# Differential attention scores: the low-key pass on 64 partitions, both components in one run of four matmuls

## The chip, the cores and the metric

The kernel runs on one core of a Trainium2 chip. Its engines are TensorE (PE; its weight loads are shown as PEld), VectorE (DVE), ScalarE (ACT), GpSimd (POOL) and SyncE (SP, which here only issues transfers). The metric is the device time of one execution in microseconds (us).

## The reference

One encoder layer is applied to two sequences, of 1024 and of 256 tokens. A state-space branch and a differential-attention branch share one input projection, and their outputs are gated and merged. What the change touches is the attention:

```python
def block(qi):
    s = jnp.einsum('bqhtd,bkhtd->bthqk', qi, k).astype(jnp.float32) * scale
    p = jax.nn.softmax(s, axis=-1)
    w = p[:, 0] - lam * p[:, 1]
    return jnp.einsum('bhqk,bkhe->bqhe', w, v)
```

There are 4 heads. Each has two components t = 0, 1 of head dimension 64, and the two softmaxes are subtracted. Query blocks have 128 rows.

## The kernel before

Every 32-bit operand of a large matmul is split into a high part and a low part (a rounded copy, and what the rounding left). In DRAM, `q_d` and `k_d` hold both parts of the rotated queries and keys. `load_head(h)` brings one head into SBUF. A query tile (`q0` for t = 0, `q1` for t = 1) stacks the 64 high rows on partitions 0 to 63 and the 64 low rows on partitions 64 to 127. A key tile holds the same 64 key rows twice, once for each half of the queries: `k00`, `k01` hold the high parts, `k10`, `k11` the low parts. One matmul over 128 partitions so gives (high q + low q) times one part of k.

A unit is one query block of one head. `unit_scores` computes its two score tiles `S0` and `S1` (128 x 1024 in PSUM, one buffer each, two banks each). For each t there is a high pass (two matmuls of 512 columns, line 924) and a low pass (two more into the same banks, line 926). Then VectorE takes the row maximum (`mx`, line 928) and scales it (line 929), ScalarE forms the exponentials `p` with the row sum (line 932), which frees the score tile, and after both components VectorE and POOL combine them (lines 937 to 940). `unit_transpose` transposes the result on TensorE (line 949) and `pair_out` multiplies it with the values (lines 961 to 963). There are 8 long units per head (1024 keys) and 2 short ones (256 keys): 32 long and 8 short in all.

The projections that only later stages need are cut into 576 steps of three matmuls, the filler (lines 706 to 708). `fill(n, ins)` puts n steps behind the instruction `ins`. Steps that the state-space and attention stages don't take are done behind them, before the gated stages, so the total number of steps is fixed. In the attention stage the order on every engine is made by a scheduler at build time, from the program and its own planning, and each engine works through its order strictly.

Transfers into the head's tiles reuse the tags `U`, `tb`, `mt`, `wcm`, `wb`, which name the SBUF slots: in the profile's rows `hU`, `htb`, `hmt`, `hwcm`, `hwb`. `S<-hmt,hU` is the low pass of t = 0 and `S<-hwb,htb` that of t = 1.

Earlier, line 440 issues very small matmuls that use 32 columns of the array. The rows give the part of the array used as rows*columns: `128*32` there, `32*128` on lines 275 and 276, `128*128` nearly everywhere else.

Of the kernel before, what the change touches and what calls it, by code (L numbers as in the profile page):

```python
# [11 lines left out]
F32 = mybir.dt.float32  # L12
# [10 lines left out]
LL = 1024  # L23
LS = 256
NT = LL + LS
# [101 lines left out]
def kernel(  # L127
# [6 lines left out]
    V, G, A, PE, SP = nc.vector, nc.gpsimd, nc.scalar, nc.tensor, nc.sync  # L134
# [3 lines left out]
    def dram(shape, dtype, name):  # L138
        return tc.dram_tile(shape, dtype, name=name)
# [7 lines left out]
    q_d = [dram([2, 2, 128, NT], F32, f"q_d{i}") for i in range(2)]  # L147
    k_d = [dram([2, 2, 128, NT], F32, f"k_d{i}") for i in range(2)]
# [27 lines left out]
    def after(ins):  # L176
        return tc.issue_after(ins.ins) if ins else ExitStack()
# [543 lines left out]
    def fill(steps, ins=None):  # L721
        with after(ins):
            for _ in range(steps):
                next(filler, None)
# [4 lines left out]
    with ExitStack() as p2:  # L729
# [20 lines left out]
        def load_wb(b):  # L750
            wb = (sp_ if b % 2 else sl).tile([128, 2, NB, 128], F32, tag="wb", name="wb")
            SP.dma_start(wb, wb_d[b])
            return wb
# [81 lines left out]
        with tc.manual_schedule(engines={mybir.EngineType.PE, mybir.EngineType.SP}):  # L835
# [10 lines left out]
            for b in range(NBLK):  # L846
                q = b // 2
# [22 lines left out]
    with ExitStack() as p3:  # L870
        ap = p3.enter_context(tc.tile_pool(name="att", bufs=1, reuse_waits="tile"))
        ps_s = p3.enter_context(tc.tile_pool(name="ps_s", bufs=1, space=PSUM, reuse_waits="tile"))
# [3 lines left out]
        def load_head(h):  # L876
            pr, cb = h // 2, (h % 2) * 2
            big = lambda tag, b: sl.tile([128, NT], F32R, tag=tag, name=f"h{tag}", bufs=b)
            sml = lambda tag, b: sl.tile([128, LL], F32R, tag=tag, name=f"h{tag}", bufs=b)
            q0, k00, q1, vh = big("U", 2), big("tb", 2), big("tb", 2), big("U", 2)  # L880
            k10, k01, k11, vl, rest = sml("mt", 2), sml("wcm", 2), sml("wb", 1), sml("mt", 2), sml("wcm", 2)
            part = lambda i: rest[:, i * LS:(i + 1) * LS]
            v3 = lambda t: t.rearrange("p (k e) -> p k e", e=128)

            def load_q(t, q):
                rows = slice((cb + t) * 32, (cb + t) * 32 + 32)
                for s in range(2):
                    for f in range(2):
                        o = s * 64 + f * 32
                        SP.dma_start(q[o:o + 32].bitcast(F32), q_d[pr][s, f, rows])  # L890

            def load_k(t, hl, k, c0, n):
                rows = slice((cb + t) * 32, (cb + t) * 32 + 32)
                for s in range(2):
                    for f in range(2):
                        o = s * 64 + f * 32
                        SP.dma_start(k[o:o + 32].bitcast(F32), k_d[pr][hl, f, rows, c0:c0 + n])

            load_q(0, q0)
            load_k(0, 0, k00, 0, NT)  # L900
            load_k(0, 1, k10, 0, LL)
            load_q(1, q1)
            load_k(1, 0, k01, 0, LL)
            load_k(1, 1, k11, 0, LL)
            SP.dma_start(v3(vh).bitcast(F32), vh_d[h])
            SP.dma_start(v3(vl).bitcast(F32), vl_d[h][:, 0:8])
            load_k(0, 1, part(0), LL, LS)
            load_k(1, 0, part(1), LL, LS)
            load_k(1, 1, part(2), LL, LS)
            SP.dma_start(v3(part(3)).bitcast(F32), vl_d[h][:, 8:10])  # L910
            return (([q0[:, :LL], q1[:, :LL]], [k00[:, :LL], k01], [k10, k11], v3(vh)[:, 0:8], v3(vl)),
                    ([q0[:, LL:], q1[:, LL:]], [k00[:, LL:], part(1)], [part(0), part(2)],
                     v3(vh)[:, 8:10], v3(part(3))))

        def unit_scores(hd, qi, nk, fu):
            qs, kh, kl = hd[:3]
            pt = []
            sm = ap.tile([128, 2], F32, tag="sm", name="sm", bufs=2)
            for t in range(2):
                S = ps_s.tile([128, LL], F32, tag=f"S{t}", name=f"S{t}")  # L920
                qw = qs[t][:, qi * 128:qi * 128 + 128]
                cks = [(c, min(512, nk - c)) for c in range(0, nk, 512)]
                for c, n in cks:
                    PE.matmul(S[:, c:c + n], qw, kh[t][:, c:c + n], start=True, stop=False)  # L924
                for c, n in cks:
                    last = PE.matmul(S[:, c:c + n], qw, kl[t][:, c:c + n], start=False, stop=True)  # L926
                mx = ap.tile([128, 1], F32, tag=f"mx{t}", name=f"mx{t}", bufs=2)
                V.tensor_reduce(mx, S[:, :nk], axis=AX.X, op=ALU.max)  # L928
                V.tensor_scalar(mx, mx, -1.0 / math.sqrt(HD), None, op0=ALU.mult)  # L929
                p = ap.tile([128, LL], F32, tag=f"p{t}", name=f"p{t}", bufs=3 - t)  # L930
                with tc.issue_after(tables.ins):
                    A.activation(p[:, :nk], S[:, :nk], AF.Exp, bias=mx, scale=1.0 / math.sqrt(HD),  # L932
                                 accum_out=sm[:, t:t + 1])
                pt.append(p)
                fill(fu[t], last if fu[t] else None)
            rs = ap.tile([128, 2], F32, tag="rs", name="rs", bufs=2)
            V.reciprocal(rs, sm)  # L937
            V.tensor_tensor(rs[:, 1:2], rs[:, 1:2], nlam, op=ALU.mult)
            G.tensor_scalar(pt[0][:, :nk], pt[0][:, :nk], rs[:, 0:1], 1.0, op0=ALU.mult, op1=ALU.mult)  # L939
            V.scalar_tensor_tensor(pt[0][:, :nk], pt[1][:, :nk], rs[:, 1:2], pt[0][:, :nk], op0=ALU.mult, op1=ALU.add)  # L940
            return pt[0]
# [71 lines left out]
        for h in range(NH):  # L1013
            parts = load_head(h)
            for pi in range(5):
                nk = LL if pi < 4 else LS
                fl = F_LONG if pi < 4 else F_SHORT
                hd = parts[pi // 4]
                wTh = ap.tile([128, 8, 256], F32R, tag="wTh", name="wTh", bufs=2)
                wTl = ap.tile([128, 8, 256], F32R, tag="wTl", name="wTl", bufs=2)  # L1020
                for qi in range(2):
                    w = unit_scores(hd, (pi % 4) * 2 + qi, nk, fl)
                    if prev:
                        finish(prev, fl[2])
                    else:
                        fill(fl[2])
                    fill(fl[3])
                    prev = (h, pi, qi, w, hd, wTh, wTl)
# [123 lines left out]
    for grp in range(2):  # L1152
# [4 lines left out]
        wb = load_wb(0)  # L1157
        for f in range(8):
            bh, bl = wb
            if f < 7:  # L1160
                wb = load_wb(f + 1)
# [13 lines left out]
            last = split_into(mh[:, f], ml[:, f], s1)  # L1175
# [75 lines left out]
```

## Time and profile before

| | us |
|---|---|
| median of 3 runs (1124.25 to 1127.57) | 1126.07 |
| the profiled execution | 1127.2 |
| its span, first to last instruction | 1125.1 |
| TensorE busy | 1067.2 (95%) |
| VectorE busy | 801.0 (71%) |
| ScalarE busy | 462.5 (41%) |
| attention stage, about 457 to 778 | 321 |

The profiled execution is 2.1 us longer than its span, and 1.1 us above the median. A matmul's duration in the rows includes the time its result takes to come out. What a matmul costs in a packed stream is the distance from its start to the next start.

### The profile page before, as it was taken

The numbers are of one execution on the slowest core, as the hardware profiler recorded it, in microseconds if no ns is written. First come the engines' busy times: TensorE is split into PE (matmuls) and PEld (weight loads), VectorE is DVE, ScalarE is ACT, GpSimd is POOL, SyncE is SP. The second block draws the span as 40 slices with busy tenths as digits, with TensorE's granted clock in tenths as the row PEclk, the third lists the DMA queues.
The fourth block names the chain that finished last, engine by engine and source line by source line (L and its number), as shares of the span: only waits on it lengthen the run. The fifth ranks groups of instructions, "written<-read, shape, count | busy, mean of one in ns | idle before, by whom it ended". The sixth has DMA issues, their size and how long they took to land.

```text
span 1125.1 us, 18000 instructions
## 1 busy us (share of the span) xinstructions
PE 1067.2 (95%) x6479; PEld 987.1 (88%) x6479; DVE 801.0 (71%) x1533; ACT 462.5 (41%) x927; POOL 354.8 (32%) x437
## 2 busy tenths in 40 slices
PE   5999799999989999999999999999999999998997
PEld 4878588788979988898999998989999999998997
DVE  5998997888579999478677777766442675666524
ACT  4453222332312121455555645554453445544332
POOL 2447999511032333122122222212141003520032
PEclk9999899999999999999999999999999999999999
DMA  7745453654596676615416316311645975569112
GB/s 212 170 141 188 142 174 117 209 166 156 173 282 174 205 202 168 177 51 150 141 47 169 122 47 186 114 40 60 210 124 174 292 230 128 167 194 270 48 57 94
DMA packets 186154, 173.59 MB, mean 154 GB/s; under 512 B 32721, under 2 KB 161745, under 8 KB 186066
## 3 DMA queue, kind: packets, MB, share of 16 engines
q1 hardware_dynamic: 150738, 144.13, 43.6%
q10 hardware_dynamic: 35328, 28.32, 7.9%
q8 instruction: 51, 0.84, 0.3%
q14 instruction: 37, 0.30, 0.1%
HBM read 113.71 MB, written 58.69 MB: 153 GB/s over the span
## 4 chain that ended last, share of the span: by engine, by line
PE 47%; DVE 18%; DMA 7%; ACT 4%; issue 3%; POOL 2%; SPq 0%; ACTq 0%; POOLq 0%; DVEq 0%
PE mm L706 5%; PE mm L707 5%; PE mm L708 5%; PE xb L1058 3%; PE xb L1059 3%; PE xb L1060 3%; PE pb L246 2%; PE pb L248 2%; PE pb L247 2%; DVE z L797 2%; DVE z L798 2%; PE S L924 2%; DMA yt<-ya_d 2%; PE S L926 2%; DVE mx L928 2%
## 5 line engine op out<-in xcount | busy, mean ns | idle before, releaser
L706 PE MATMUL mm<-hTh,wh 128*128 128x424 f32 (+1 forms) x576 | 212.2, 368 | 6.3 <-ACT zo L712 6.3
L708 PE MATMUL mm<-hTh,wl 128*128 128x424 f32 (+1 forms) x576 | 206.1, 358 | 0.0
L707 PE MATMUL mm<-hTl,wh 128*128 128x424 f32 (+1 forms) x576 | 206.0, 358 | 0.0
L706 PEld LDWEIGHTS mm<-hTh,wh 128*128 128x128 f32 x576 | 109.2, 190 | 12.6 <-ACT zo L712 8.1
L707 PEld LDWEIGHTS mm<-hTl,wh 128*128 128x128 f32 x576 | 109.2, 190 | 4.6
L708 PEld LDWEIGHTS mm<-hTh,wl 128*128 128x128 f32 x576 | 109.0, 189 | 3.4
L928 DVE TENSOR_REDUCE mx<-S 128x1 f32<-128x1024 f32 (+1 forms) x80 | 84.2, 1057 | 38.9 <-PE S L926 38.7
L939 POOL TENSOR_SCALAR p<-p,rs 128x1024 f32<-128x1024 f32 (+1 forms) x40 | 41.7, 1042 | 205.0 <-DVE rs L937 194.2
L246 PE MATMUL pb<-hTh,wh 128*128 128x512 f32 (+1 forms) x288 | 105.7, 367 | 0.0
L247 PE MATMUL pb<-hTl,wh 128*128 128x512 f32 (+1 forms) x288 | 105.1, 365 | 0.0
L932 ACT ACTIVATE p<-S,mx 128x1024 f32<-128x1024 f32 (+1 forms) x80 | 79.2, 992 | 63.0 <-DVE mx L929 53.8
L248 PE MATMUL pb<-hTh,wl 128*128 128x512 f32 (+1 forms) x288 | 103.9, 361 | 0.4 <-DVE wl L240 0.4
L240 POOL TENSOR_TENSOR wl<-wst,wh 128x1024 fp32r<-128x1024 f32 x24 | 64.3, 2679 | 126.5 <-ACT wh L239 51.7
L1191 PE MATMUL tr<-wqh,mh 128*128 128x256 f32 x320 | 89.7, 280 | 1.5 <-DVE o L1195 1.3
L1192 PE MATMUL tr<-wql,mh 128*128 128x256 f32 x320 | 89.3, 279 | 0.0
L1193 PE MATMUL tr<-wqh,ml 128*128 128x256 f32 x320 | 89.0, 279 | 0.0
L248 PEld LDWEIGHTS pb<-hTh,wl 128*128 128x128 f32 x288 | 54.6, 190 | 9.3 <-DVE wl L240 0.9
L246 PEld LDWEIGHTS pb<-hTh,wh 128*128 128x128 f32 x288 | 54.7, 190 | 8.6
L1191 PEld LDWEIGHTS tr<-wqh,mh 128*128 128x128 f32 x320 | 60.1, 188 | 2.4 <-DVE o L1195 2.4
L247 PEld LDWEIGHTS pb<-hTl,wh 128*128 128x128 f32 x288 | 54.6, 190 | 8.4
L1198 POOL TENSOR_TENSOR o<-o,finB 128x256 f32<-128x256 f32 x30 | 27.9, 934 | 103.8 <-ACT jk L1197 103.8
L1192 PEld LDWEIGHTS tr<-wql,mh 128*128 128x128 f32 x320 | 60.1, 188 | 0.0
(387 smaller groups left out, 2793.4 us busy)
## 6 DMA issues: line engine op xcount, KB each, us to landing
wst<-in_w_in_dram ACTq DMA_DIRECT2D x24, 512.0 KB, 4.0
wst<-in_w_in_dram SPq DMA_DIRECT2D x16, 512.0 KB, 4.8
wst<-in_w_branch_dram SPq DMA_DIRECT2D x32, 256.0 KB, 4.4
wqs<-in_w_out_dram SPq DMA_DIRECT2D x16, 512.0 KB, 3.8
tt_d<-tt SPq DMA_DIRECT2D x16, 320.0 KB, 2.6
tb<-tt_d SPq DMA_DIRECT2D x8, 640.0 KB, 5.1
zt<-gs_d SPq DMA_DIRECT2D x16, 320.0 KB, 4.3
x<-in_x_sample_dram SPq DMA_DIRECT2D x8, 512.0 KB, 4.6
```

Of the source, the lines that this page charges most:

```text
L240: e.tensor_tensor(lv, st, hv, op=ALU.subtract)
L246: PE.matmul(ps[:, :n], wh[:, k, :], hTh[:, k, c0:c0 + n], start=(k == 0), stop=False)
L247: PE.matmul(ps[:, :n], wh[:, k, :], hTl[:, k, c0:c0 + n], start=False, stop=False)
L248: PE.matmul(ps[:, :n], wl[:, k, :], hTh[:, k, c0:c0 + n], start=False, stop=(k == KD - 1))
L706: PE.matmul(ps[:, :n], wh[:, k, :], hTh[:, k, c0:c0 + n], start=(k == 0), stop=False)
L707: PE.matmul(ps[:, :n], wh[:, k, :], hTl[:, k, c0:c0 + n], start=False, stop=False)
L708: PE.matmul(ps[:, :n], wl[:, k, :], hTh[:, k, c0:c0 + n], start=False, stop=(k == KD - 1))
L928: V.tensor_reduce(mx, S[:, :nk], axis=AX.X, op=ALU.max)
L932: A.activation(p[:, :nk], S[:, :nk], AF.Exp, bias=mx, scale=1.0 / math.sqrt(HD), accum_out=sm[:, t:t + 1])
L1191: PE.matmul(ps[:, :256], mh[:, k, ts_], oh_[:, k], start=(k == 0), stop=False)
L1192: PE.matmul(ps[:, :256], mh[:, k, ts_], ol_[:, k], start=False, stop=False)
L1193: PE.matmul(ps[:, :256], ml[:, k, ts_], oh_[:, k], start=False, stop=(k == 7))
```

## The change

The low pass of the long units leaves out the product of the low queries with the low keys. It uses the high queries only, so 64 partitions of operands instead of 128. Its four matmuls (two halves of the keys for each of two components) are put on alternating halves of the partitions: keys 0 to 511 on partitions 0 to 63, keys 512 to 1023 on partitions 64 to 127. The high passes of both components come first, then the four low matmuls in one run, held behind the last high matmul. The filler of both components now waits for the last low matmul. Short units keep their 128-partition low pass.

For this `load_head` builds other tiles. `klo` (slot `mt`) has the low keys of both components once each, split over the partition halves. The high queries must stand on both halves, so `q1` is stacked the other way round (low rows first), and `qx` (slot `wb`) holds the two missing copies.

```diff
-            k10, k01, k11, vl, rest = sml("mt", 2), sml("wcm", 2), sml("wb", 1), sml("mt", 2), sml("wcm", 2)
+            klo, k01, qx, vl, rest = sml("mt", 2), sml("wcm", 2), sml("wb", 1), sml("mt", 2), sml("wcm", 2)
...
+            def load_klo(t):
+                rows = slice((cb + t) * 32, (cb + t) * 32 + 32)
+                for s in range(2):
+                    for f in range(2):
+                        o = s * 64 + f * 32
+                        SP.dma_start(klo[o:o + 32, t * 512:t * 512 + 512].bitcast(F32),
+                                     k_d[pr][1, f, rows, s * 512:s * 512 + 512])
+
-            load_q(0, q0)
+            load_q(0, q0, 0, 0)
+            load_q(0, q0, 64, 1)
             load_k(0, 0, k00, 0, NT)
-            load_k(0, 1, k10, 0, LL)
-            load_q(1, q1)
+            load_klo(0)
+            load_q(0, qx, 64, 0, LL)
+            load_q(1, q1, 64, 0)
+            load_q(1, q1, 0, 1)
             load_k(1, 0, k01, 0, LL)
-            load_k(1, 1, k11, 0, LL)
+            load_klo(1)
+            load_q(1, qx, 0, 0, LL)
...
+            his = ((q0[0:64], qx[64:128]), (qx[0:64], q1[64:128]))
+            los = [[(his[t][s], klo[64 * s:64 * s + 64, t * 512:t * 512 + 512]) for s in range(2)] for t in range(2)]
...
-            for t in range(2):
-                S = ps_s.tile([128, LL], F32, tag=f"S{t}", name=f"S{t}")
+            cks = [(c, min(512, nk - c)) for c in range(0, nk, 512)]
+            Ss = [ps_s.tile([128, LL], F32, tag=f"S{t}", name=f"S{t}") for t in range(2)]
+            for t, S in enumerate(Ss):
                 qw = qs[t][:, qi * 128:qi * 128 + 128]
-                cks = [(c, min(512, nk - c)) for c in range(0, nk, 512)]
                 for c, n in cks:
-                    PE.matmul(S[:, c:c + n], qw, kh[t][:, c:c + n], start=True, stop=False)
-                for c, n in cks:
-                    last = PE.matmul(S[:, c:c + n], qw, kl[t][:, c:c + n], start=False, stop=True)
+                    hi_last = PE.matmul(S[:, c:c + n], qw, kh[t][:, c:c + n], start=True, stop=False)
+                if nk < LL:
+                    last = PE.matmul(S[:, :nk], qw, kl[t], start=False, stop=True)
+            if nk == LL:
+                for t, S in enumerate(Ss):
+                    for (c, n), (qh_, kl_) in zip(cks, kl[t]):
+                        with after(hi_last):
+                            last = PE.matmul(S[:, c:c + n], qh_[:, qi * 128:qi * 128 + 128], kl_, start=False, stop=True)
+            for t, S in enumerate(Ss):
                 mx = ap.tile([128, 1], F32, tag=f"mx{t}", name=f"mx{t}", bufs=2)
```

The order on TensorE at the fifth long unit of the first head, before. `S_5307` is its S0 and `S_5338` its S1; `tr<-ident,p` are the transposes of an earlier unit.

```order
L924 MATMUL S_5307<-htb,hU 128x512 x2
L926 MATMUL S_5307<-hmt,hU 128x512 x2
L949 MATMUL tr<-ident,p_5147 128x128 x8
...
L924 MATMUL S_5338<-hwcm,htb 128x512 x2
L926 MATMUL S_5338<-hwb,htb 128x512 x2
```

The same unit in the changed kernel, where `S_5311` is S0 and `S_5312` is S1, the high pass is line 936 and the low pass line 943.

```order
L936 MATMUL S_5311<-htb,hU 128x512 x2
L936 MATMUL S_5312<-hwcm,htb 128x512 x2
L943 MATMUL S_5311<-hmt,hU 128x512
L943 MATMUL S_5311<-hmt,hwb 128x512
L943 MATMUL S_5312<-hmt,hwb 128x512
L943 MATMUL S_5312<-hmt,htb 128x512
L706 MATMUL mm<-hTh,wh 128x424
```

The two components stood 8 transposes and 18 filler matmuls apart and now stand together, with the low pass of both behind them. From the low pass of S_5311 to the next unit's S0 there are now 21 filler matmuls, 8 transposes and two matmuls of the normalization; before, from the low pass of S_5307, there were 8 transposes, 18 and then 3 filler matmuls, the four matmuls of S_5338 and the same two of the normalization.

VectorE at the same unit, before: the row maximum of S0 (`mx_5312`), its scaling, and what stands up to the maximum of S1 (`mx_5343`).

```order
L928 TENSOR_REDUCE mx_5312<-S_5307 128x1
L929 TENSOR_SCALAR mx_5312<-mx_5312 128x1
L937 RECIPROCAL rs<-sm 128x2
L938 TENSOR_TENSOR rs<-rs,nlam 128x1
L953 TENSOR_TENSOR wTl<-tr,wTh 128x4x128 x2
L940 SCALAR_TENSOR_TENSOR p_5244<-p_5270,rs,p_5244 128x1024
L928 TENSOR_REDUCE mx_5343<-S_5338 128x1
```

VectorE there in the changed kernel (`mx_5321` for S0, `mx_5347` for S1):

```order
L946 TENSOR_REDUCE mx_5321<-S_5311 128x1
L958 SCALAR_TENSOR_TENSOR p_5253<-p_5274,rs,p_5253 128x1024
L946 TENSOR_REDUCE mx_5347<-S_5312 128x1
L947 TENSOR_SCALAR mx_5321<-mx_5321 128x1
L971 TENSOR_TENSOR wTl<-tr,wTh 128x4x128
```

The scaling of S0's maximum, for which ScalarE's exponentials wait, stood right behind the maximum and now stands behind the combination of the unit before and behind the maximum of S1.

SP's queue where the second head is loaded, in the changed kernel. Before, 12 transfers of 32x1024 (`hmt`, `hwcm` and `hwb`, four each) stood ahead of the `ya_d` store.

```order
L895 DMA hwcm<-k_d_91 32x1024 x2
L902 DMA hmt<-k_d_91 32x512 x4
L888 DMA hwb<-q_d_89 32x1024 x2
L895 DMA hwcm<-k_d_91 32x1024 x2
L902 DMA hmt<-k_d_91 32x512 x4
L888 DMA hwb<-q_d_89 32x1024
L1015 DMA ya_d_95<-ya 128x512
L888 DMA hwb<-q_d_89 32x1024
L895 DMA htb<-k_d_91 32x1280
```

There are 16 transfers in place of 12 between the head's last long unit and the loads that wait for its short units, and one of them stands behind the `ya_d` store.

## Rows read from the trace of the kernel before

**Rows 1.** Attention stage: stretch, its length, busy us per engine (instructions), clock, DMA.

```profile
457.00:778.00 321.00, 312.24 (x1821) 289.87 (x1821) 234.51 (x425) 172.31 (x351) 73.25 (x52) 0.99 0.37 108
```

**Rows 2.** Timeline, PE, second head: start, us, engine, line, operation.

```profile
596.00 0.62 PE L924 MATMUL S<-htb,hU 128*128 128x512 f32 x2
596.47 0.62 PE L926 MATMUL S<-hmt,hU 128*128 128x512 f32 x2
596.93 0.35 PE L706 MATMUL mm<-hTh,wh 128*128 128x432 f32 x1
597.12 0.36 PE L707 MATMUL mm<-hTl,wh 128*128 128x432 f32 x1
```

**Rows 3.** All low passes of long units (line 926): count, ns min/median/max, starts.

```profile
L926 PE MATMUL S<-hmt,hU x64: 387/396/628, 458.1 to 759.5; 128*128 128x512 f32 x64
L926 PE MATMUL S<-hwb,htb x64: 387/394/403, 461.3 to 762.8; 128*128 128x512 f32 x64
```

**Rows 4.** Timeline, PE, around one run of the 32-column matmuls.

```profile
294.61 0.28 PE L248 MATMUL pb<-hTh,wl 128*128 128x256 f32 x1
294.82 0.25 PE L440 MATMUL tr<-Cr,Bb 128*32 128x16 f32 x4
294.90 0.23 PE L440 MATMUL tr<-Cna,Bb 128*32 128x16 f32 x4
295.06 0.39 PE L246 MATMUL pb<-hTh,wh 128*128 128x256 f32 x1
295.28 0.28 PE L247 MATMUL pb<-hTl,wh 128*128 128x256 f32 x1
295.40 0.28 PE L248 MATMUL pb<-hTh,wl 128*128 128x256 f32 x1
```

**Rows 5.** Timeline, PEld (weight loads), same place.

```profile
294.49 0.19 PEld L248 LDWEIGHTS pb<-hTh,wl 128*128 128x128 f32 x1
294.82 0.15 PEld L440 LDWEIGHTS tr<-Cr,Bb 128*32 128x32 f32 x4
```

**Rows 6.** Timeline, PE, the only matmuls on 32 rows of the array.

```profile
29.17 0.28 PE L547 MATMUL mm<-Wvh,hTl 128*128 128x256 f32 x1
29.38 0.30 PE L275 MATMUL tr<-ident,an 32*128 32x32 f32 x2
```

**Rows 7.** Waits of PEld in the attention stage: us in total, times, longest.

```profile
PEld S L924 <- ACT p L932: 9.3, 12, 2.4
```

**Rows 8.** Timeline, PE, the first unit's low pass of S0 ends.

```profile
458.53 0.36 PE L706 MATMUL mm<-hTh,wh 128*128 128x432 f32 x1
```

**Rows 9.** Timeline, DVE, behind it; in brackets idle time before and releaser.

```profile
458.73 1.22 DVE L928 TENSOR_REDUCE mx<-S 128x1 f32<-128x1024 f32 x1 [6.74 <-PE S L926]
459.99 0.15 DVE L929 TENSOR_SCALAR mx<-mx 128x1 f32<-128x1 f32 x1
```

**Rows 10.** Timeline, ACT, behind that.

```profile
460.24 1.11 ACT L932 ACTIVATE p<-S,mx 128x1024 f32<-128x1024 f32 x1 [1.17 <-DVE mx L929]
```

**Rows 11.** Line 940: ns min/median/max.

```profile
L940 DVE SCALAR_TENSOR_TENSOR p<-p,rs,p x40: 470/1276/3202, 467.3 to 777.1; 128x1024 f32<-128x1024 f32 x32, 128x256 f32<-128x256 f32 x8
```

**Rows 12.** Timeline, PE, transposes.

```profile
561.99 1.06 PE L949 MATMUL tr<-ident,p 128*128 128x128 f32 x8 [0.52 <-DVE mx L929]
562.81 0.44 PE L706 MATMUL mm<-hTh,wh 128*128 128x424 f32 x1
```

**Rows 13.** Four us behind the longest wait: columns as in Rows 1.

```profile
472.00:476.00 4.00, 4.00 (x20) 3.74 (x19) 1.83 (x4) 1.03 (x2) 0.00 (x0) 0.67 0.00 0
```

**Rows 14.** Timeline, SP queue, load of the second head.

```profile
518.11 1.81 SPq L897 DMA_DIRECT2D hwb<-k_d  x4
524.32 0.34 SPq L997 DMA_DIRECT2D ya_d<-ya  x1
530.47 2.24 SPq L890 DMA_DIRECT2D htb<-q_d  x4
```

**Rows 15.** Transfers into q1's tile: count, KB each, median us to landing.

```profile
htb<-q_d SPq DMA_DIRECT2D x12, 160.0 KB, 5.2
```

**Rows 16.** Timeline, PE, the second head's first S0.

```profile
537.49 0.64 PE L924 MATMUL S<-htb,hU 128*128 128x512 f32 x2
```

More of the change, by code (lines that the diff above doesn't have):

```diff
@@ L880, in load_head, with load_q @@
             q0, k00, q1, vh = big("U", 2), big("tb", 2), big("tb", 2), big("U", 2)
-            k10, k01, k11, vl, rest = sml("mt", 2), sml("wcm", 2), sml("wb", 1), sml("mt", 2), sml("wcm", 2)
+            klo, k01, qx, vl, rest = sml("mt", 2), sml("wcm", 2), sml("wb", 1), sml("mt", 2), sml("wcm", 2)
             part = lambda i: rest[:, i * LS:(i + 1) * LS]
             v3 = lambda t: t.rearrange("p (k e) -> p k e", e=128)
-            def load_q(t, q):
+            def load_q(t, q, o, hl, n=NT):
                 rows = slice((cb + t) * 32, (cb + t) * 32 + 32)
[L887 to L890, printed above, removed]
+                for f in range(2):
+                    SP.dma_start(q[o + f * 32:o + f * 32 + 32].bitcast(F32), q_d[pr][hl, f, rows, 0:n])
             def load_k(t, hl, k, c0, n):
@@ L897, in load_k @@
                         SP.dma_start(k[o:o + 32].bitcast(F32), k_d[pr][hl, f, rows, c0:c0 + n])
-            load_q(0, q0)
+            def load_klo(t):
+                rows = slice((cb + t) * 32, (cb + t) * 32 + 32)
+                for s in range(2):
+                    for f in range(2):
+                        o = s * 64 + f * 32
[3 more added lines that the diff above has]
+            load_q(0, q0, 64, 1)
             load_k(0, 0, k00, 0, NT)
-            load_k(0, 1, k10, 0, LL)
-            load_q(1, q1)
+            load_klo(0)
+            load_q(0, qx, 64, 0, LL)
+            load_q(1, q1, 64, 0)
+            load_q(1, q1, 0, 1)
             load_k(1, 0, k01, 0, LL)
-            load_k(1, 1, k11, 0, LL)
+            load_klo(1)
+            load_q(1, qx, 0, 0, LL)
             SP.dma_start(v3(vh).bitcast(F32), vh_d[h])
@@ L910, in load_head @@
             SP.dma_start(v3(part(3)).bitcast(F32), vl_d[h][:, 8:10])
-            return (([q0[:, :LL], q1[:, :LL]], [k00[:, :LL], k01], [k10, k11], v3(vh)[:, 0:8], v3(vl)),
+            his = ((q0[0:64], qx[64:128]), (qx[0:64], q1[64:128]))
+            los = [[(his[t][s], klo[64 * s:64 * s + 64, t * 512:t * 512 + 512]) for s in range(2)] for t in range(2)]
+            return (([q0[:, :LL], q1[:, :LL]], [k00[:, :LL], k01], los, v3(vh)[:, 0:8], v3(vl)),
                     ([q0[:, LL:], q1[:, LL:]], [k00[:, LL:], part(1)], [part(0), part(2)],
```

## The prediction

> **What bounds the kernel now.** I read the stretches first, to see which engine is full where the change works. In the attention stage TensorE is busy 312.2 of 321 us, VectorE 234.5, ScalarE 172.3 [rows 1]. The filler has a fixed number of steps and what attention does not take is done behind it, so TensorE time saved in attention comes off the end, and TensorE time added is paid there, as long as no wait grows. The timeline of TensorE comes second, for the price of a matmul in the stream: starts lie 0.23 us apart for 512 columns (596.47 to 596.93 for two) and 0.19 to 0.20 for a filler matmul of 432 [rows 2]. The low passes are 128 matmuls [rows 3], four in each of 32 long units, so 0.92 us a unit and 29.4 us in all. The list of waits comes third: TensorE's weight loads waited 9.3 us in 12 places for the exponentials that free a score tile, at most 2.4 us [rows 7]. So nearly all of the stage is a packed stream of matmuls, and two things decide: what the four low matmuls cost in the stream, and whether the score tiles still come free in time.
>
> **The low pass itself.** The number of low matmuls (4 a unit) and their columns (512) stay. Fewer partitions alone buy nothing in this count; a gain must come from two matmuls on different halves of the array running at once. No row shows that. The bounds for a pair are 0.23 us (full overlap) and 0.46 (none). I take nearly full overlap: the two of a pair share no row of the array and write different banks, and in the nearest row, the 32-column matmuls, eight loads and eight matmuls fit into 0.24 us, 0.03 each [rows 4], with four loads inside 0.15 us [rows 5]. I allow 0.01 for the second one's later start: 0.24 a pair, 0.48 for the four.
>
> Against it stands the change of the used part of the array, twice a unit. Rows 4 show such a change: the last 128*128 matmul of 256 columns starts at 294.61 and the first 128*32 at 294.82, 0.21 later, where the next one would have come 0.12 later (295.28 to 295.40) [rows 4]. That is 0.09 us lost. The only matmuls on 32 rows show the same 0.21 (29.17 to 29.38) [rows 6], so it is not a matter of columns. The weight load usually starts one matmul ahead; here it starts only with its own matmul, at 294.82 [rows 5], so the load is not hidden either. Its price is seen on the way back: the first 128*128 matmul behind the run starts at 295.06 and the next at 295.28, 0.22 instead of 0.12: 0.10 for a load of 128 columns [rows 4]. The delay on the way back can't be told from the small matmuls in the 0.24 between 294.82 and 295.06; it lies between 0 and 0.24, and I take the 0.09 of the way in. One unit then costs 0.09 + 0.10 + 0.48 + 0.09 + 0.10 = 0.86 us against 0.92: a gain of 0.06, or 1.9 us for 32 units.
>
> The Trainium skill has a rule that speaks against the change: "TensorEngine Tiling (Array Packing)", section "Key Properties", says that changing the tiling mode drains TensorE. The rows agree and give the size, 0.09 us; with no drain at all the sum would be 64 x 0.09 = 5.8 us lower.
>
> **When the scores come free.** S0's row maximum now starts behind the low pass of both components. The old loop from the end of S0's low pass: it ends at 458.53, where the next matmul starts [rows 8]; the maximum starts at 458.73, its scaling at 459.99 [rows 9]; the exponentials run from 460.24 to 461.35 [rows 10]. That is 2.8 us. In the new order of VectorE the combination of the unit before (1.28 us by its median) [rows 11] and the maximum of S1 (1.26 from start to start) [rows 9] stand ahead of the scaling, so the loop takes 2.8 + 1.28 + 1.26 = 5.35 us. What covers it on TensorE at the fifth unit is 21 filler matmuls (4.1 us), 8 transposes (0.82, from 561.99 to 562.81) [rows 12] and two normalization matmuls (0.24): 5.16 us. Before, the four matmuls of S1 lay there too: 6.1 us against 2.8. So the cover of 3.3 us goes to about zero, and S0 is 0.2 us late. Behind the waiting matmul stand the transposes and the filler, which all wait with it. Where the value matmuls (24 x 0.12 = 2.8 us) stand in the gap, nothing is late. By the order two units of each head have the tight form (the second and the fifth), 8 in all: 8 x 0.2 = 1.6 us. The bounds: 0, since the old waits of 9.3 us [rows 7] lie in the same places and some of them may go, and 16 us more, if each of the 8 met the longest combination (3.20 instead of 1.28) [rows 11]. I take 1.0, since of the waits of before a part must go when the order changes.
>
> **Loads.** Per head 4 transfers more are issued, with the same number of bytes. SP takes 0.45 us for one (1.81 for four), 1.8 us a head. SP finished `hwb` at 519.92 and stood until the store at 524.32 [rows 14], 4.4 us, so this is hidden; without that room it would delay the loads behind by up to 1.8 us. One transfer into `hwb` now stands behind that store; its low pass is more than 10 us later. q1 is needed sooner: it was issued from 530.47 to 532.71 [rows 14] and lands 5.2 us later [rows 15], at 537.9. S0 of the new head starts at 537.49 [rows 16], and in the new order ten value matmuls, two transposes and nine filler matmuls (1.2 + 0.2 + 1.8 us) stand between it and the high pass of S1, which so comes at 540.7. That leaves 2.8 us; nothing is late.
>
> The sum: -1.9 + 1.0 = -0.9 us. Against the profiled execution, 1127.2 (span 1125.1 and 2.1 around it), that is 1126.3; this execution was 1.1 us above the median of 1126.07, so for a median I predict 1125.2, rounded to 1125. A measurement of this kernel can tell about 0.3% (3.4 us) from no change, so this is no change.
>
> **The rivals.**
> First, slower: the pairs do not overlap. Place: line 943, every long unit. The four matmuls then take 0.92 plus the same 0.38 for the two changes of the array's part: 1.30, 0.38 more than before, 12.2 us in all, with the 1.0 of the waits about 1139. For it: no row shows two matmuls sharing the array by rows, and the weights of a pair may load one behind the other. Against it: only the closeness of the small matmuls. It decides from the pair's time on: the change breaks even at (0.92 - 0.38) / 2 = 0.27 us a pair, and is slower by 0.3% from 0.32.
>
> Second, waits grow: the tight hand-overs miss more than 0.2 us. Three of the 8 meeting a combination of 3.2 us would add 5.8 us, and a stop of two us has a price behind it: in the four us behind the longest wait the mean granted clock was 0.67 [rows 13], part of the time at 1.2 GHz instead of 2.4, 1.3 us of work lost. With -1.9 + 1.0 that is 1131 without such a price, 1135 with it. For it: VectorE's order puts two long operations ahead of the scaling. Against it: these places are few, and median durations just fit.
>
> Third, the changes of the array's part are cheaper between 128*128 and 64*128 than rows 4 show, because the weight loads are hidden. If the two loads (0.20) cost nothing, the gain is 0.26 a unit, 8.3 us, and the time 1118 to 1119; with both changes free 0.44 a unit, 14 us, 1113. For it: the tile still spans all columns, and the other half's load may run ahead. Against it: rows 4 and 6 agree on the late start, for columns and for rows.
>
> The Trainium skill, same page, section "Theoretical Speedup", gives up to twice the speed for a contraction of 64 or fewer; taken alone it means this last 1113. "TensorE: Matmul & The Clock Gate", Part 3, reports matmuls on different row groups running at once, 3.07 times for four; no run here shows it.
>
> **How the numbers follow.** Overlap with the price of rows 4, near balance: 0.45, own range 1120 to 1130. No overlap: 0.22. Waits grow: 0.13. Cheaper changes: 0.20. The range from 1118 to 1140 holds the first and third case, most of the second and the nearer half of the fourth. Faster by over 0.3%: the fourth and a small part of the first, 0.28. Slower: the second, most of the third, a little of the first, 0.35. Within: 0.37.
>
> **What would show it.** In the changed kernel's timeline the two low matmuls of a pair start less than 0.05 us apart if they overlap, 0.23 if not; the run of four should take about 0.5 from its first streaming, and the first filler behind it should start about 0.85 us after the last high matmul has streamed. Starts 0.2 us apart in all four would be the first rival. A list of waits with clearly more than 9.3 us for the exponentials would be the second. A weight load of the low pass that starts while the last high matmul streams would be the third. The prediction is wrong altogether if the stage's length changes for another reason, such as a head whose loads come late.

## The result and the profile after

| | before | after |
|---|---|---|
| median of the runs compared, us | 1126.82 (4 runs) | 1144.24 (1143.52 to 1145.6, 4 runs) |
| ratio, 95% interval | | 1.0158 (1.0137 to 1.018) |
| span of the profiled execution, us | 1125.1 | 1143.8 |
| mean granted clock in it | 0.987 | 0.987 |

The changed kernel is 17.4 us slower; 1125 with a range of 1118 to 1140 was predicted. I read the stretches first, as for [rows 1]. Columns: stretch, its length, busy us of PE, PEld, DVE, ACT and POOL (instructions), clock, DMA share, GB/s.

```profile
457.00:796.00 339.00, 320.07 (x1836) 274.50 (x1835) 232.20 (x426) 172.94 (x353) 71.08 (x52) 0.99 0.36 103
```

The attention stage is 18 us longer, 339 instead of 321 for about as many matmuls (1836, before 1821). VectorE and ScalarE have nearly the same work (232.2 and 172.9 us, before 234.5 and 172.3). TensorE stands still 18.9 us there instead of 8.8. Its modelled busy time is longer too, 320.1 us instead of 312.2; matmuls whose weights came late stand in the rows with longer durations (0.73 us at 602.15 below, 0.62 at 601.34). The mean clock is the same. So most of the time was lost in TensorE's stream inside the stage.

Next, the low pass, which the forecast was about. Timeline of TensorE, changed kernel, one long unit of the second head:

```profile
601.34 0.62 PE L936 MATMUL S<-htb,hU 128*128 128x512 f32 x2
602.15 0.73 PE L936 MATMUL S<-hwcm,htb 128*128 128x512 f32 x2 [0.19 <-ACT p L950]
602.81 0.50 PE L943 MATMUL S<-hmt,hU 64*128 64x512 f32 x1
602.81 0.73 PE L943 MATMUL S<-hmt,hwb 64*128 64x512 f32 x2
603.15 0.39 PE L943 MATMUL S<-hmt,htb 64*128 64x512 f32 x1
603.47 0.46 PE L706 MATMUL mm<-hTh,wh 128*128 128x432 f32 x1
603.77 0.36 PE L707 MATMUL mm<-hTl,wh 128*128 128x432 f32 x1
```

The L943 row with x2 holds one matmul of each pair. The two matmuls of a pair start together, at 602.81, so they overlap. The second pair follows 0.34 us later, at 603.15, the first filler matmul 0.32 behind it, the second filler matmul 0.30 behind that (0.20 in a packed stream, [rows 2]). The low pass works, and at the forecast's price (below).

What is wrong stands one line above. S0's two full matmuls start at 601.34, so S1's should follow at 601.81; they come at 602.15, and the bracket names the exponentials that free S1's tile. Now the list of waits in the stage: engine, tile and line, releaser, us in total, times, longest. A late matmul can stand in it twice, under PE and under PEld, its weight load.

```profile
PEld S L936 <- ACT p L950: 19.0, 28, 1.0
PEld S L943 <- issue: 11.7, 32, 0.4
PE S L936 <- ACT p L950: 9.6, 21, 0.8
PEld mm L706 <- issue: 8.8, 24, 0.4
PE S L936 <- DMA htb<-k_d: 2.3, 2, 1.4
PE S L936 <- DMA htb<-q_d: 1.3, 1, 1.3
```

The weight loads' wait for exponentials was 9.3 us in 12 places [rows 7]; it is 19.0 in 28. None is longer than 1.0 us: many small delays, not a few large ones. New are waits of a head's first S0 for its loads. The two rows with "issue" I read as the changes of the array's part: the first counts 32, one for each long unit.

By tile, the 28 are these: 7 are S0 of long units (2.6 us, five of them 0.15 to 0.22), 13 are S1 of long units (9.4 us), and 8 stand in the short units (7.0 us).

Why S1 is late is seen on VectorE and ScalarE ahead of that unit. The low passes of the unit before end where the next matmul starts, at 594.13.

```profile
594.13 0.66 PE L967 MATMUL tr<-ident,p 128*128 128x128 f32 x4
594.45 0.68 DVE L971 TENSOR_TENSOR wTl<-tr,wTh 128x512 fp32r<-128x512 f32 x1
595.05 1.21 DVE L946 TENSOR_REDUCE mx<-S 128x1 f32<-128x1024 f32 x1
596.18 1.27 DVE L958 SCALAR_TENSOR_TENSOR p<-p,rs,p 128x1024 f32<-128x1024 f32 x1
597.37 1.21 DVE L946 TENSOR_REDUCE mx<-S 128x1 f32<-128x1024 f32 x1
598.50 0.68 DVE L971 TENSOR_TENSOR wTl<-tr,wTh 128x512 fp32r<-128x512 f32 x1
599.10 0.20 DVE L947 TENSOR_SCALAR mx<-mx 128x1 f32<-128x1 f32 x2
```

```profile
599.27 1.11 ACT L950 ACTIVATE p<-S,mx 128x1024 f32<-128x1024 f32 x1
600.38 0.62 ACT L1007 ACTIVATE rr<-ya 128x512 f32<-128x512 f32 x1
600.90 1.11 ACT L950 ACTIVATE p<-S,mx 128x1024 f32<-128x1024 f32 x1
```

From its maximum on, S0's loop takes 5.33 us here (595.05 to 600.38). The forecast's 5.35 counts from the end of the low pass, and from there it is 6.25 (594.13 to 600.38), since VectorE comes to the maximum only behind other work. Over the long units this loop takes 4.3 to 7.2 us, 5.23 at the median. S0's tile is free at 600.38 and is asked for at 601.34, so S0 is not late. S1's tile is free only at 602.0, 1.6 us after S0's, because its exponentials stand behind S0's on ScalarE, here with one normalization operation between. TensorE asks for it only 0.47 us after S0's. Before, the low pass of S0 and part of the filler lay between the two.

Last, the change of heads. SP's queue and TensorE at the second head of the changed kernel:

```profile
531.21 0.30 SPq L895 DMA_DIRECT2D htb<-k_d  x1
531.61 1.80 SPq L888 DMA_DIRECT2D hU<-q_d  x4
533.46 2.10 SPq L895 DMA_DIRECT2D htb<-k_d  x3
535.66 2.37 SPq L888 DMA_DIRECT2D htb<-q_d  x4
```

```profile
530.90 0.28 PE L936 MATMUL S<-htb,hU 128*128 128x256 f32 x1
540.69 0.70 PE L936 MATMUL S<-htb,hU 128*128 128x512 f32 x2 [1.29 <-DMA htb<-q_d]
```

The old head's last reading of its k tile is the short unit's S0 at 530.90; the new k load is issued at 531.21 and is complete on the queue at 535.56. TensorE has run out of other work at 539.4 and waits 1.29 us. The bracket names a load of q1, but the transfer that lands just ahead of S0 is the last one of k, at 540.55; the first of q1 lands at 541.27. In the kernel before, the last reading stands here, and the new S0 at 537.49 [rows 16]:

```profile
526.51 0.28 PE L924 MATMUL S<-htb,hU 128*128 128x256 f32 x1
```

That is 10.98 us later, without a wait for a load. Here TensorE comes to that point 8.5 us after the last reading (530.90 to 539.40). That alone does not make the wait: before, the last k transfer landed 7.95 us after the last reading (at 534.46), so 0.5 us would have been left. In the changed kernel it takes 9.65 us to land, 1.7 more. At the two other changes of heads the landing takes 1.1 and 0.8 us more than before.

To size the parts I took, for each pair of neighbouring matmuls from the first S0 to the last normalization matmul of the attention, the distance of their starts less the distance in a packed stream (0.235 us for 512 columns, 0.198 and 0.194 for 432 and 424, 0.1185 for 256, 0.099 for 128), and summed it by what follows what. In us, against the kernel before, with the kernels of the experiments that are read the same way:

| kernel | within the low pass | around it, and filler | S0 to S1 | first S0 of a head | other waits ahead of S | ahead of transposes | rest | sum |
|---|---|---|---|---|---|---|---|---|
| changed | -11.6 | +9.4 | +6.2 | +4.1 | +3.2 | +3.8 | +0.3 | +15.5 |
| order alone | -0.4 | +0.4 | +6.0 | +4.7 | +3.0 | +3.2 | +0.8 | +17.8 |
| rows alone | -14.5 | +17.0 | +0.5 | 0.0 | -1.5 | +1.1 | +1.7 | +4.3 |
| filler between | -11.9 | +11.8 | +0.7 | +2.4 | +5.7 | -3.3 | +20.2 | +25.7 |
| changed, short units +16 steps | -11.1 | +7.7 | +6.4 | 0.0 | -0.8 | +1.3 | +3.0 | +6.5 |
| changed, +80 steps | -11.7 | +6.4 | +3.3 | 0.0 | -7.4 | -2.7 | +1.5 | -10.6 |
| before, +80 steps | -0.2 | -0.3 | +0.1 | +3.2 | -8.0 | -2.8 | +0.1 | -7.9 |

So the row form gains 2.2 us net in the changed kernel (-11.6 + 9.4), and the waits take 17.3 (6.2 + 4.1 + 3.2 + 3.8). Behind the stage another 2.9 us are lost: from the last normalization matmul to the end it is 328.6 us (815.2 to 1143.8), before 325.7 (799.4 to 1125.1).

### The profile page after: what moved, and what is told of

Same layout as the page of the kernel before. It is cut to its first block, busy times and chain, and to the rows that moved or that the text cites. A ratio compares the mean times of both kernels' runs of the same rounds, so it can differ in the third digit from the quotient of the medians.

```text
span 1143.8 us, 18022 instructions
## 1 busy us (share of the span) xinstructions
PE 1073.8 (94%) x6479; PEld 969.1 (85%) x6479; DVE 801.1 (70%) x1533; ACT 462.1 (40%) x927; POOL 352.6 (31%) x437
## 4 chain that ended last, share of the span: by engine, by line
PE 39%; DVE 18%; DMA 10%; ACT 7%; issue 3%; POOL 3%; SPq 1%; ACTq 0%; POOLq 0%; DVEq 0%
PE mm L706 4%; PE mm L707 4%; PE mm L708 4%; ACT p L950 3%; DVE z L798 3%; DVE z L797 3%; PE xb L1076 2%; PE xb L1077 2%; PE xb L1078 2%; PE pb L246 2%; PE pb L248 2%; PE pb L247 2%; PE S L936 2%; DMA yt<-ya_d 2%; DVE mx L946 2%
## 5 line engine op out<-in xcount | busy, mean ns | idle before, releaser
L706 PE MATMUL mm<-hTh,wh 128*128 128x424 f32 (+1 forms) x576 | 215.3, 374 | 5.8 <-ACT zo L712 5.8
L240 POOL TENSOR_TENSOR wl<-wst,wh 128x1024 fp32r<-128x1024 f32 x24 | 61.8, 2576 | 131.9 <-ACT wh L239 105.5
L712 ACT COPY zo<-mm 128x424 f32<-128x424 f32 (+1 forms) x72 | 36.9, 513 | 74.1 <-PE mm L708 47.7
```

Source lines behind the costliest of these rows:

```text
L240: e.tensor_tensor(lv, st, hv, op=ALU.subtract)
L706: PE.matmul(ps[:, :n], wh[:, k, :], hTh[:, k, c0:c0 + n], start=(k == 0), stop=False)
```

## The experiments

The theory: the row form gains its 2 us, and the new order of TensorE's stream loses 17 to 18. **Rival one**: the 64-row matmuls or the changes of the array's part cost it. **Rival two**: the changed loads cost it. Times are medians; the kernel before had medians of 1126.5 to 1128.4 beside them.

**Order alone.** Loads and low pass of the kernel before, in the changed order:

```diff
+            for t, S in enumerate(Ss):
...
+                    hi_last = PE.matmul(S[:, c:c + n], qw, kh[t][:, c:c + n], start=True, stop=False)
...
+                    qw = qs[t][:, qi * 128:qi * 128 + 128]
+                    for c, n in cks:
+                        with after(hi_last):
+                            last = PE.matmul(S[:, c:c + n], qw, kl[t][:, c:c + n], start=False, stop=True)
```

> The kernel before with its own loads and its low passes on 128 rows, but in the changed order: full passes of both components, the four low matmuls behind them in one run, all filler behind the last low matmul, both components of a short unit one behind the other. There is no change of the array's part in it. Theory: the loss is made by this order. Then the time is that of the changed kernel plus the 0.06 us a long unit that the row form gains, 1144 + 2, so 1142 to 1148, and TensorE waits for the exponentials (S from p) about as long as in the changed kernel, near 29 us together. Rival one, the 64-row matmuls or the changes of the array's part cost it: 1124 to 1130. Rival two, the loads: the head's change waits for no load of k or q, and the time is 1124 to 1130.

Measured: 1144.92, ratio 1.0155 (1.0131 to 1.0179). Its list of waits and the unit that answers to the one above:

```profile
PE S L924 <- ACT p L939: 8.6, 20, 0.8
PE S L924 <- DMA htb<-q_d: 3.1, 2, 1.8
...
PEld S L924 <- ACT p L939: 18.7, 28, 1.1
```

```profile
602.82 0.62 PE L924 MATMUL S<-htb,hU 128*128 128x512 f32 x2
603.63 0.73 PE L924 MATMUL S<-hwcm,htb 128*128 128x512 f32 x2 [0.19 <-ACT p L939]
604.20 0.63 PE L932 MATMUL S<-hmt,hU 128*128 128x512 f32 x2
604.67 0.62 PE L932 MATMUL S<-hwb,htb 128*128 128x512 f32 x2
```

With no 64-row matmul, no change of the array's part and the old loads, the whole loss is there, down to S1 late by the same 0.34 us (0.81 between 602.82 and 603.63) and about as many waits (28 and 20, there 28 and 21). Both rivals fall. A head's first S0 also waits for its loads with the old transfers, and the last k transfer takes as long to land (9.67 us at the second head), so the added transfers are not the reason; what is, stays open.

From the first S0 to the last normalization matmul it is 359.5 us, 2.3 more than in the changed kernel (357.2). The two kernels have the same 1942 matmuls there in the same order, so they can be compared place by place. In each of the 32 long units the changed one gains 0.05 to 0.12 us at the low pass, 2.15 in all, and all other places together differ by 0.1. That is the row form by itself. In the whole time only 0.7 us of it is seen, less than these runs can tell.

**Rows alone.** The 64-row passes and their loads, component by component as before, each with its own filler:

```diff
-            for t, S in enumerate(Ss):
+            for t in range(2):
+                S = ps_s.tile([128, LL], F32, tag=f"S{t}", name=f"S{t}")
...
-            if nk == LL:
-                for t, S in enumerate(Ss):
+                else:
                     for (c, n), (qh_, kl_) in zip(cks, kl[t]):
```

> The changed kernel with its own loads and the low pass on 64 rows, but component by component as in the kernel before: two full matmuls, one pair on 64 rows, this component's filler, then the other component. The array's part changes four times a long unit instead of twice. Theory: the order makes the loss. Then the old waits come back and only the price of the pairs is added: a pair with both changes costs 0.09 + 0.10 + 0.24 + 0.09 + 0.10 = 0.62 against 0.46 for two full matmuls, 0.16 more, 64 times, 10 us: 1137, between 1133 and 1140. Rival one, the changes of the array's part or the row form make the loss of 17 us with 64 changes: with 128 of them the loss is twice that, near 1160. Rival two, the loads: 1144 or more, the 17 us stay and the pairs come on top (1150).

Measured: 1133.51, ratio 1.0064 (1.0042 to 1.0087), 6 us over the kernel before. One pair in its timeline:

```profile
597.25 0.62 PE L936 MATMUL S<-htb,hU 128*128 128x512 f32 x2
597.81 0.49 PE L942 MATMUL S<-hmt,hU 64*128 64x512 f32 x1
597.81 0.49 PE L942 MATMUL S<-hmt,hwb 64*128 64x512 f32 x1
598.23 0.47 PE L706 MATMUL mm<-hTh,wh 128*128 128x432 f32 x1
598.54 0.35 PE L707 MATMUL mm<-hTl,wh 128*128 128x432 f32 x1
```

The second full matmul starts at 597.48 (0.23 behind 597.25). The pair comes 0.33 later, 0.10 more than in a stream; the filler 0.42 behind it, which is 0.24 for the pair, 0.10 for its weights and 0.08; and the next one 0.31 behind, 0.11 too much. From 597.48 to 598.54 it is 1.06 us; two full matmuls instead would make 0.90 (3 x 0.235 + 0.198). So a pair costs 0.16 more than it saves, as expected. In the table the first two columns hold only +2.5 of it, since behind 22 of the 64 pairs something other than filler follows. Compared place by place with the kernel before (again the same order), the pairs and the matmuls beside them cost 8.8 us, and the other places are 4.5 us shorter. So the stage is 4.3 us longer, and 6 us were measured and not 10. The waits of PE and PEld for the exponentials are 3.9 and 5.9 us; before, TensorE's was 5.8 and that of the weight loads 9.3 [rows 7]. More than half of the 4.5 us is one place: the longest wait of before is 2.07 us on TensorE, here 0.61, and the slow clock behind it [rows 13], worth another 1.1 us of the 4.5, is absent. With 128 changes of the array's part the kernel is 11 us faster than with 64 in the other order; rival one falls again, and rival two with it, since these are the changed loads.

**Short units in the old order.** Long units as changed:

```diff
+            if nk < LL:
+                for t in range(2):
+                    S = ps_s.tile([128, LL], F32, tag=f"S{t}", name=f"S{t}")
+                    softmax(t, S, scores(t, S))
...
```

> The changed kernel, but with the short units in the old order (each component's full and low matmul with its own filler behind it); the long units are as in the changed kernel. Theory: of the 17 us some 4 lie at the head's change (S0 of the new head waits for q and k, 1.1 to 1.5 us, three times) and some 3 in the score tiles of the short units, and both come from the short units' order, since the last tile is freed later in it: 1137 to 1140. Rival one (array's part, long units alone): 1144, within 2. Rival two (loads): 1144, and S0 of a new head still waits for its loads over 1 us.

Measured: 1142.78, ratio 1.0135 (1.0117 to 1.0153); 1.5 us back of the 4 to 7 expected, less than these runs can tell. A new head's S0 still waits for its loads (1.7 and 1.3 us in the list of waits): here six filler matmuls and four transposes stand ahead of the second short unit's S0, where the kernel before has them behind it, so the cover is short again. My account of the head's change, that the last tile is freed too late, was off: what counts is how much work stands between the last reading of the old tile and the first of the new, against the time that the load takes.

**More filler in the short units**, 16 steps of three matmuls, taken from behind the stage; in the changed kernel and in the kernel before:

```diff
-F_SHORT = (3, 2, 3, 0)
+F_SHORT = (4, 2, 4, 0)
```

> The changed kernel with the same 16 filler steps more in the short units, without the priority. Theory: S0 of a new head no longer waits 1.1 to 1.5 us for its loads (4.1 us), short units' tiles come in time (2 to 3 us): 1137 to 1140, if nothing is lost behind the stage. Rival one: 1142 to 1146. Rival two, the loads: 4 us back, 1140.

> The kernel before with the same 16 filler steps more in the short units. Control for the two others: it has no waits for loads at the head's change, so it gains at most 2 us in the stage, and shows what 48 matmuls fewer behind the stage cost: 1125 with room there, up to 1137 without.

Measured: changed kernel 1139.6, ratio 1.0109 (1.008 to 1.0138); kernel before 1125.27, ratio 0.9985 (0.9971 to 0.9999). All waits of S on exponentials or DMA in the changed kernel's stage are now:

```profile
PEld S L936 <- ACT p L950: 16.3, 25, 1.8
PE S L936 <- ACT p L950: 8.3, 17, 1.4
```

No S waits for a load any more, and 4.6 us come back where the kernel before gains 1.3. So the head's change is a matter of cover, and worth about 3 to 4 us. The waits for exponentials are left, most of them in the long units.

**More filler in all units** (80 steps), in both kernels. The sum of work stays:

```diff
-F_LONG = (4, 1, 2, 0)
-F_SHORT = (3, 2, 3, 0)
+F_LONG = (6, 1, 2, 0)
+F_SHORT = (4, 2, 4, 0)
```

> The changed kernel with more filler in each unit: six steps instead of four in a long unit's first part, and four and four instead of three and three in a short unit (80 steps, 240 matmuls, taken from what is done behind the stage; the total stays). Theory: the score tiles and the loads are late by less than 1.2 us in nearly all places, and two steps are 1.2 us, so most of the 17 us come back: 1127 to 1132. Rival one, the array's part: its cost stays, 1142 to 1146. Rival two, loads: 2 us at most come back at the head's changes, 1140 to 1144.

> The kernel before with the same extra filler. Control: it has 15.5 us of stalls in TensorE's stream, of which some 8 are late score tiles and transposes; 1119 to 1127. Theory: with enough cover the two orders differ by the row form alone, the changed kernel 2 us faster than this one; rival one: the changed kernel stays 10 us or more slower than this one.

Measured: 1159.66, ratio 1.0278 (1.0263 to 1.0293), and 1160.85, ratio 1.0286 (1.0268 to 1.0303). As a time the first expectation is missed by 28 us, and for both kernels alike. The reason lies behind the stage, in the first of these kernels (columns as above):

```profile
838.00:898.00 60.00, 36.32 (x180) 32.07 (x179) 31.04 (x35) 28.16 (x39) 13.88 (x8) 0.75 0.75 237
```

TensorE is busy 36 of 60 us there, at a mean granted clock of 0.75: the filler that covered the start of the next stage has been used up. I had not looked at what that filler covers. But inside the stage the pair of kernels answers most of the question. The changed kernel's waits:

```profile
PEld S L936 <- ACT p L950: 2.8, 5, 0.9
```

The exponentials cost 2.8 us in 5 places instead of 19.0 in 28, while the changes of the array's part stay (11.3 us in 32 places in the same list). And the stage is 377.1 us against 379.8 in the kernel before with the same filler. So with enough cover the 17 us are gone. Which form is then ahead, these two traces don't show. The kernel before lost more than the 2.7 us at one place, where a head's first S0 waited for its load and the clock fell behind it (columns of the second row as above):

```profile
630.49 0.70 PE L924 MATMUL S<-htb,hU 128*128 128x512 f32 x2 [3.02 <-DMA htb<-q_d]
631.00:635.00 4.00, 4.00 (x14) 3.61 (x13) 1.98 (x5) 0.00 (x0) 0.48 (x1) 0.57 0.87 224
```

That is 3.0 us and 1.7 of work lost ((1 - 0.57) x 4). The trace of the changed kernel has no such place, and the medians differ by 1.2 us, less than these runs can tell.

**Filler between the two full passes.** Four steps moved ahead of S1:

```diff
+                if nk == LL and t == 0:
+                    fill(fu[0], hi_last)
...
-                fill(fu[t], last if fu[t] else None)
+                if nk < LL or t:
+                    fill(fu[t], last if fu[t] else None)
```

> The changed kernel, but the first part of a long unit's filler (four steps, 12 matmuls, 2.3 us) stands between the full pass of S0 and the full pass of S1 instead of behind the low passes. Theory: S1 is late because only S0's two full matmuls lie ahead of it in a unit; the stalls between S0's and S1's full passes (6.2 us more than in the kernel before) go. But the same 2.3 us are taken from S0's cover, whose loop of 2.8 to 5.4 us is then late: waits before S0 grow by 0 to 1.5 us in each of 32 units. 1138 if S0 has room, 1150 to 1165 if it has none; I take 1150. Rivals one and two (array's part, loads): 1142 to 1146, since neither changes.

Measured: 1157.21, ratio 1.0249 (1.0225 to 1.0274). The full passes of the long units, grouped by form (count | busy us, mean ns | idle time ahead and what ended it):

```profile
L936 PE MATMUL S<-htb,hU 128*128 128x512 f32 x64 | 22.0, 425 | 6.5 <-ACT p L952 3.1 <-DMA htb<-k_d 1.4 <-issue 0.6
L936 PE MATMUL S<-hwcm,htb 128*128 128x512 f32 x64 | 20.4, 393 | 0.0
```

S1 (the second row) waits no more, as expected: its stall falls from 6.2 to 0.7 us over the kernel before. The time goes up all the same, and mostly elsewhere than I said: S0 loses some more, but 20 us come up where value matmuls and normalization follow the filler (in the table "rest"). Value matmuls and normalization wait 10.8 us for VectorE there (TensorE's list of waits), in the changed kernel not at all: the 12 filler matmuls behind the low passes had covered this. The same 2.3 us of cover can't be had at two places.

**Priority** for maximum, scaling and exponentials, in the changed kernel, in the kernel before, and with the 16 steps in the short units:

```diff
+                with tc.high_priority():
                     mx = ap.tile([128, 1], F32, tag=f"mx{t}", name=f"mx{t}", bufs=2)
...
```

> The changed kernel, but maximum, scaling and exponentials of a unit are issued with priority, so on VectorE and ScalarE they stand ahead of other work that is ready at the same place. Theory: the score tiles come free late because the combination of the unit before and other work stand ahead of them; then the waits for the exponentials (28.6 us on both lists) fall by a third or more and the time is 1134 to 1141. Rivals one and two (array's part, loads): 1142 to 1146. If the priority pushes the transposes' work back instead, transposes wait for VectorE and the time is above 1146.

> The kernel before with the priority for maximum, scaling and exponentials that the changed kernel had in the experiment before this one. Theory: the priority helps only where a score tile comes free too late. The kernel before waited 15.1 us for exponentials on both lists (its overlaps counted once some 8), the changed one 28.6, so it gains less here than the 7 us there: 1122 to 1127. If the priority were worth 7 us here too, the waits of the changed order would have no part in it: 1120.

> The changed kernel with priority for maximum, scaling and exponentials, and with 16 filler steps more in the short units alone (four and four instead of three and three; 9.6 us taken from behind the stage). Theory: the priority gives back 7 us as before; the steps in the short units cover the new head's loads and the short units' tiles, 4 to 6 us more. Behind the stage the filler (290 matmuls) must cover until the next stage's data come, and shrinks by 48; where that cover is short, up to 9.6 us are lost again. 1131 to 1136 with room behind, 1137 to 1142 without. Rivals one and two: 1142 and more.

Measured: 1137.28, ratio 1.011 (1.0064 to 1.0156); 1128.22, ratio 1.0001 (0.9987 to 1.0015); and 1141.2, ratio 1.0129 (1.011 to 1.0148). In the first the waits for exponentials fall to 13.5 and 5.8 us from 19.0 and 9.6, and the kernel before gains nothing, where 1122 to 1127 was expected. But the trace of the first is that of its slowest run (1148.03, the three others 1136.5 to 1137.5), and with the 16 steps the priority gives nothing (1141.2 against 1139.6). So part of the loop's length may be VectorE's order; these runs show neither that nor how much.

**Cover taken from ahead of the stage**: the kernel with priority and 16 steps, and 16 filler steps fewer ahead of the state scan:

```diff
-S_PRE, S_LEAD, S_MID, S_END = 22, 10, 13, 4
+S_PRE, S_LEAD, S_MID, S_END = 6, 10, 13, 4
```

> The experiment with priority and 16 steps more in the short units, and those 16 steps taken from the filler that stands ahead of the stage (6 instead of 22 ahead of the first block of the state scan), so that behind the stage all 290 matmuls are left. Theory: 1129 to 1134, if the first block has no need of the cover; if it has, its engines stand still for up to 9.6 us and the time is 1139 to 1143.

Measured: 1148.54, ratio 1.0189 (1.0164 to 1.0214). Between 300 and 400 us TensorE is busy 85.8 us at a clock of 0.93, before 93.0 at 0.97, and its waits from 300 to 457 us are 20.6 us, in the kernel with priority and 16 steps alone 12.1: the first block needed that cover. The upper case came true, and 5 us more than it. These 16 steps were not spare.

No version of the change comes out ahead of the kernel before. The best time is that of the kernel before with 16 filler steps more in its short units, 1.3 us, at the edge of what can be told.

## Why the prediction was wrong

**The low pass: right.** The forecast for a unit was 0.09 + 0.10 + 0.48 + 0.09 + 0.10 = 0.86 us. The rows give 0.10 of delay on the way in (597.48 to 597.81 in the kernel with the rows alone, less 0.235); 0.34 from pair to pair, 0.24 and 0.10 for the first pair's weights; 0.32 to the filler, 0.24 and 0.08 on the way back; and 0.10 too much to the next one: 0.86. The -1.9 us came as -2.2. The part left between 0 and 0.24, the way back, is 0.08, nearly as on the way in. The first rival (no overlap) and the third (cheaper changes) are both excluded, by 602.81 twice and by 603.15 and 603.77.

The Trainium skill, "TensorEngine Tiling (Array Packing)", section "Key Properties", says that different tiles load and multiply in parallel and that a change of mode drains the engine. The trace agrees with both: the pair's matmuls start in the same hundredth of a microsecond (602.81), as do their weight loads, and a change costs 0.08 to 0.10 us. Whether this time is a drain, no row tells.

**When the scores come free: the step that failed.** It is the term of 1.0 us for the waits, made of the sentence "S0 is 0.2 us late" alone. For S0 the sentence was about right: behind the fifth unit of each head the next S0 is late by 0.22 us, and in the last three heads the loop there takes 5.36 us (forecast 5.35). Behind the second unit it is late in the first head alone (0.54), and that head has two more late S0 (1.00 and 0.15). Three things were left out. First, S1: its exponentials end 1.1 to 1.9 us behind S0's, and in the new order S1 is asked for 0.47 us behind S0. 13 of the 32 long units have a late S1: +6.2 us, the largest part. Second, the short units, whose components now stand together too; most of the +3.2 us ahead of other S lies there. Third, the transposes: they wait for VectorE more than before, +3.8 us. So the wait term is 13.2 us where 1.0 stood.

**Loads: failed for the first S0.** "Nothing is late" was worked out for q1 and S1. The 2.8 us of spare were S1's; S0's own k and q, released by the short unit's S0, had 2.5 us less time at the second head, and there its last k transfer landed 1.7 us later after the release than before: +4.1 us over three changes of heads. The four transfers more are not the reason: the order alone, with the old loads, loses 4.7 there.

The second rival had the right direction, but its mechanism was a few large misses and a slow clock behind them. What happened is many of about 1 us at most, at an unchanged mean clock. The condition set down for it, clearly more than 9.3 us of waits for exponentials, was met with 19.0, as was the last one, a head whose loads come late.

What stays open: the 2.9 us behind the stage, why the new head's loads take longer to land, and how much of the loop is VectorE's order.

## What to carry to other kernels

When two tiles that were asked for in turn are asked for together, work out the hand-over for the later one: the chain behind both still runs in turn, but the second consumer's head start is gone. Cover that stood between two uses is not regained by standing behind both. Before filler is moved for it, look up what it covers where it stands: 16 steps taken from behind the stage cost nothing that shows, but 80 from there, 16 from ahead of the stage and 4 from behind the low passes each cost more than they gave.

## What the runs showed of the hardware

Waits of one size were followed by a slower clock at one place and not at others. At 539.40 the changed kernel's TensorE stood for 1.29 us, and the granted clock of the stretch from 500 to 550 us is 1.00. In the short units of the third head two shorter waits follow each other, and behind them the clock falls, to 1.2 GHz from 699 to 701 us (columns as above):

```profile
696.46 0.38 PE L936 MATMUL S<-htb,hU 128*128 128x256 f32 x1 [0.80 <-ACT p L950]
697.56 0.39 PE L936 MATMUL S<-hwcm,htb 128*128 128x256 f32 x1 [0.53 <-DMA hwcm<-k_d]
697.00:699.00 2.00, 1.47 (x6) 1.31 (x6) 1.95 (x6) 2.00 (x7) 1.20 (x1) 0.73 0.72 153
699.00:701.00 2.00, 2.00 (x8) 1.87 (x7) 2.00 (x6) 0.47 (x2) 0.16 (x1) 0.50 0.69 220
```

That is 1.5 us of work lost ((1 - 0.73) x 2 + (1 - 0.50) x 2), more than the waits themselves (1.33). But two waits of nearly the same length stand at the same place of the first and the second head (0.80 and 0.50, 0.79 and 0.53), and the clock stays at 1.00; the first head's:

```profile
524.90 0.38 PE L936 MATMUL S<-htb,hU 128*128 128x256 f32 x1 [0.80 <-ACT p L950]
525.99 0.38 PE L936 MATMUL S<-hwcm,htb 128*128 128x256 f32 x1 [0.50 <-DMA hwcm<-k_d]
524.00:530.00 6.00, 4.70 (x26) 4.26 (x26) 5.72 (x13) 4.07 (x12) 1.12 (x1) 1.00 0.62 167
```

So the fall behind one of the three is not explained by these waits. In the kernel before a slower stretch stood behind its longest wait [rows 13], and with 80 steps more it stood behind the wait of 3.02 us.

The other surprise is that a slower stream hides waits: the kernel with the rows alone pays 0.16 us for each of 64 pairs, about 10 us by that price, and is only 6 us slower.
